# A gated product streamed through one core: the first tile in pieces, and an early copy on the scalar engine's DMA queue

## The chip, the core and the metric

The kernel runs on one core of one Trainium2 chip. The metric is the device time of one execution in microseconds (us). Before the change the median of three runs is 933.64 us (933.28 to 933.91).

The core's engines each follow their own list of instructions and meet through semaphores: ACT (the scalar engine), DVE (the vector engine), POOL, PE (no work here) and SP, which here only issues transfers. Transfers between device memory (DRAM) and on-chip memory (128 partitions) are carried by 16 DMA engines. SP and ACT each have a DMA queue of their own; both feed the same 16 engines. In the trace SP's queue is q1 and ACT's is q10.

## The reference

```python
# x: 8192 x 8192, float32
def reference(x):
    a, b = np.split(x, 2, axis=-1)
    return a * (1 / (1 + np.exp(-b)))     # 8192 x 4096, float32
```

Each row of x holds 4096 values of a and then 4096 of b; the output is a times the sigmoid of b. 268 MB are read and 134 MB written, and each value is used once.

## The kernel before

**Tiles.** A tile is 256 rows of x: two neighbouring rows in each of the 128 partitions (`R = 2`), so that a partition's part of a load is one run of 64 KB in DRAM, and its part of a store one run of 32 KB. There are 32 tiles. Inputs and outputs have two buffers each (`x_sb0`, `x_sb1`, `o_sb0`, `o_sb1`), and tile i uses buffer i mod 2.

**A tile's work.** SP issues the load (L51). ACT replaces b by its sigmoid in place (L66), DVE multiplies a by it into the output buffer (L80), and ACT issues the store (L90). Most tiles are one ACT and one DVE instruction over two rows of 4096 columns. Two tiles are cut. Tile 0 is loaded as two DMAs, one for each row of a partition, and worked as the whole first row and then three parts of the second (1024, 1024 and 2048 columns); it is stored whole. The last tile is loaded whole and worked in four parts of 2048 columns, which SP stores as four DMAs.

**Order.** The program has no scheduler; `trace` (L100 to L116) writes down the order, and the semaphores do the rest:

- `loaded0` and `loaded1` count a tile's load for each buffer, and `row` the second row of tile 0. Each DMA adds 16 when it has landed. The first sigmoid of a tile waits for `loaded`.
- `ready0` and `ready1` count, for each buffer, the first sigmoid of a tile and the landing of stores. The first multiply of tile i waits for both: its sigmoid, and the store of tile i - 2 that empties the output buffer. Later pieces of a tile wait for `sigmoid`.
- `product` counts multiplies. Load i + 2 waits until the multiplies of tile i are done, and so does the store of tile i.

A waiting instruction holds up what stands behind it on the same engine. On SP that is the order of the loads; on ACT the store of tile i stands between the sigmoids of tile i and those of tile i + 1.

**The beginning.** The program opens with a barrier between the engines (L175, L157 in the trace). `_launch_early` (L133) takes the first load, the first row of tile 0, out of the body and puts it ahead of SP's drain of that barrier, so that it is issued before the engines have met. All other DMAs are issued behind the barrier: SP goes on with the second row of tile 0 and the whole of tile 1, and ACT loads its table for the sigmoid.

**The end.** `close` (L118) drains ACT, DVE and SP; POOL waits for them and for the store of the last tile but one, and clears the semaphores. SP waits for the last four stores (L130).

Of the kernel before, what the change touches and what calls it, by code (L numbers as in the profile page):

```python
# [1 line left out]

# [4 lines left out]

P = 128
R = 2
SLOTS = 2  # L10


class _Program:

    def __init__(self, nc, x, out):
        self.nc = nc
        fp32 = mybir.dt.float32
        n_rows, n_cols = x.shape  # L30
        self.half = n_cols // 2
        self.n_tiles = n_rows // (P * R)
        self.x = x.rearrange("(n p r) m -> n p (r m)", p=P, r=R)
        self.out = out.rearrange("(n p r) m -> n p (r m)", p=P, r=R)
        self.xs = [nc.alloc_sbuf_tensor(f"x_sb{s}", [P, R * n_cols], fp32).ap() for s in range(SLOTS)]
        self.os = [nc.alloc_sbuf_tensor(f"o_sb{s}", [P, R * self.half], fp32).ap() for s in range(SLOTS)]
        self.loaded = [nc.alloc_semaphore(f"loaded{s}") for s in range(SLOTS)]
        self.ready = [nc.alloc_semaphore(f"ready{s}") for s in range(SLOTS)]
        self.product = nc.alloc_semaphore("product")
        self.sigmoid = nc.alloc_semaphore("sigmoid")  # L40
        self.row = nc.alloc_semaphore("row")
        self.arrived = nc.alloc_semaphore("arrived")
        self.last = nc.alloc_semaphore("last")
        self.to_ready, self.stored = [0] * SLOTS, [0] * SLOTS
        self.products = self.sigmoids = self.lasts = 0
        self.done = {}

    def load(self, i, rows=slice(0, R), landed=None):
        s = i % SLOTS
        part = slice(rows.start * 2 * self.half, rows.stop * 2 * self.half)  # L50
        ins = self.nc.sync.dma_start(out=self.xs[s][:, part], in_=self.x[i][:, part])  # L51
        ins.then_inc(landed or self.loaded[s], 16)
        if i >= SLOTS:
            ins._wait_ge(self.product, self.done[i - SLOTS])
        return ins

    def work(self, i, pieces):


        nc, s = self.nc, i % SLOTS  # L60
        rows = self.xs[s].rearrange("p (r h m) -> p r h m", r=R, h=2)
        packed = self.os[s].rearrange("p (r m) -> p r m", r=R)
        waits = []
        for k, (r, c) in enumerate(pieces):
            b = rows[:, r, 1, c]
            sig = nc.scalar.activation(out=b, in_=b, func=mybir.ActivationFunctionType.Sigmoid)  # L66
            if k == 0:
                sig._wait_ge(self.loaded[s], 16 * (i // SLOTS + 1))
                self.to_ready[s] += 1 + self.stored[s]
                waits.append((self.ready[s], self.to_ready[s]))  # L70
                sig.then_inc(self.ready[s], 1)
                self.stored[s] = 0
            else:
                if i == 0 and r.start == 1 and c.start == 0:
                    sig._wait_ge(self.row, 16)
                self.sigmoids += 1
                waits.append((self.sigmoid, self.sigmoids))
                sig.then_inc(self.sigmoid, 1)
        for (r, c), wait in zip(pieces, waits):
            mul = nc.vector.tensor_mul(out=packed[:, r, c], in0=rows[:, r, 0, c], in1=rows[:, r, 1, c])  # L80
            mul._wait_ge(*wait)
            mul.then_inc(self.product, 1)
            self.products += 1
        self.done[i] = self.products

    def store(self, i, lo=0, hi=None, products=None):
        s, final = i % SLOTS, i == self.n_tiles - 1
        hi = R * self.half if hi is None else hi
        queue = self.nc.sync if final else self.nc.scalar
        ins = queue.dma_start(out=self.out[i][:, lo:hi], in_=self.os[s][:, lo:hi])  # L90
        ins._wait_ge(self.product, self.done[i] if products is None else products)
        if final:
            self.lasts += 16
            ins.then_inc(self.last, 16)
        else:
            self.stored[s] += 16
            ins.then_inc(self.ready[s], 16)
        return ins

    def trace(self):  # L100

        n, half = self.n_tiles, self.half
        whole = [(slice(0, R), slice(0, half))]
        cuts = (0, half // 4, half // 2, half)
        by_row = [(slice(0, 1), slice(0, half))] + [(slice(1, 2), slice(a, b)) for a, b in zip(cuts, cuts[1:])]
        fourths = [(slice(r, r + 1), slice(h * half // 2, (h + 1) * half // 2)) for r in range(R) for h in range(2)]
        self.load(0, slice(1, 2), self.row)
        self.load(1)
        for i in range(n):
            self.work(i, fourths if i == n - 1 else whole if i else by_row)  # L110
            if i + SLOTS < n:
                self.load(i + SLOTS)
            if i < n - 1:
                self.store(i)
        for k in range(4):
            self.store(n - 1, k * half // 2, (k + 1) * half // 2, self.products - 3 + k)  # L116

    def close(self):  # L118


        nc, s = self.nc, (self.n_tiles - 2) % SLOTS
        for engine in (nc.scalar, nc.vector, nc.sync):
            engine.drain().then_inc(self.arrived, 1)  # L123
        nc.gpsimd.wait_ge(self.arrived, 3)
        nc.gpsimd.wait_ge(self.ready[s], self.to_ready[s] + self.stored[s])
        ids = sorted(h.num for h in (*self.loaded, *self.ready, self.product, self.sigmoid, self.row, self.arrived))
        assert ids == list(range(ids[0], ids[-1] + 1)) and self.last.num not in ids
        nc.gpsimd.sem_clear(range(ids[0], ids[-1] + 1))
        nc.gpsimd.drain()
        nc.sync.wait_ge(self.last, self.lasts).then_inc(self.last, -self.lasts)  # L130


def _launch_early(nc):  # L133

    SP = mybir.EngineType.SP
    entry, body = (b.instructions for b in nc.main_func.blocks[:2])
    load = next(i for i in body if i.engine == SP and i.opcode == "DMACopy")
    assert not load.sync_info.on_wait  # L140
    body.remove(load)
    where = next(k for k, i in enumerate(entry) if i.engine == SP and i.opcode == "Drain")
    entry.insert(where, load)


@with_exitstack
def kernel(
    ctx: ExitStack,
    tc: tile.TileContext,
    x: bass.AP,  # L150
    out: bass.AP,
):
    nc = tc.nc
    prog = _Program(nc, x, out)
    tc.info.no_tile_sem_insts.add(prog.load(0, slice(0, 1)).ins.name)
    tc.close()
    tc.compile()  # L157
    _launch_early(nc)
    prog.trace()
    prog.close()  # L160


# [1 line left out]
_INS = ['x']  # L164
_OUTS = [((8192, 4096), 'float32')]


# [23 lines left out]
```

## Time and profile before

The profile is of one execution. Its first instruction is SP's early load at 0.00, and its last is SP's wait for the last stores.

| what | value |
|---|---|
| median of three runs | 933.64 us |
| span of the profiled execution, first to last instruction | 932.0 us |
| moved by the DMA engines over the span | 402.67 MB, 432 GB/s |
| DVE busy, 38 instructions | 278.7 us |
| ACT busy, 39 instructions | 226.9 us |
| a sigmoid of a whole tile / of 2048 / of 1024 columns | 7.03 / 1.90 / 1.05 us |
| a multiply of a whole tile / of 2048 / of 1024 columns | 8.69 / 2.29 / 1.22 us |
| a whole load, issue to landing (median) | 42.2 us |
| a whole store, issue to landing (median) | 34.8 us |
| one of the last four stores, issue to landing (median) | 5.8 us |

How to read it: an engine's busy time says how much it works, not what the kernel waits for. DMA time from issue to landing holds the time behind other transfers on the same engines. The trace also keeps every DMA packet with its queue, start, duration and size. A packet here is one partition's run of a DMA, up to 64 KB, or one record of 4 bytes that tells a semaphore of a DMA's end; each of the 16 engines carries the packets of 8 partitions.

### The profile page before, as it was taken

To read this page: it belongs to the slowest core of one execution; us is meant where nothing else is said; L and a number is where in the kernel's file an instruction comes from. 1 tells how busy PE (TensorE), PEld (TensorE's weight loads), DVE (VectorE), ACT (ScalarE), POOL (GpSimd) and SP (SyncE) were. 2 spreads that over 40 slices of the span, in tenths; PEclk is the share of its full clock that TensorE was granted. 3 is DMA by queue.
4 is the path that set the end of the run, shared out by engine and by line. 5 is a ranking of instruction groups with operands and counts; after the bars stand their busy time and mean duration, and the time that the engine had idled before them with its cause. 6 is when DMAs were issued, how large, how long until landed. Compare 5 with 4: busy or idle time off the path is not lost.

```text
span 932.0 us, 191 instructions
## 1 busy us (share of the span) xinstructions
DVE 278.7 (30%) x38; ACT 226.9 (24%) x39; POOL 0.2 (0%) x4
## 2 busy tenths in 40 slices
DVE  2133213332133331233312333123331233312333
ACT  2133330233311333113331133311333113332033
POOL 0000000000000000000000000000000000000000
DMA  9999999999999999999999999999999999999999
GB/s 405 418 460 428 408 461 413 450 428 428 450 405 450 428 428 450 428 428 428 461 416 428 436 464 428 405 458 419 450 428 425 453 405 450 428 428 450 423 432 405
DMA packets 9793, 402.67 MB, mean 432 GB/s; under 512 B 1088, under 2 KB 1088, under 8 KB 1088
## 3 DMA queue, kind: packets, MB, share of 16 engines
q1 hardware_dynamic: 5328, 272.63, 67.7%
q10 hardware_dynamic: 4464, 130.03, 32.3%
q14 instruction: 1, 0.01, 0.0%
HBM read 268.44 MB, written 134.22 MB: 432 GB/s over the span
## 4 chain that ended last, share of the span: by engine, by line
DMA 73%; DVE 15%; ACT 12%; DVEq 0%; issue 0%; SPq 0%
DMA x_sb<-in_x_dram 73%; DVE o_sb L80 15%; ACT x_sb L66 12%; DVEq L123 0%; SPq L51 0%
## 5 line engine op out<-in xcount | busy, mean ns | idle before, releaser
L80 DVE TENSOR_TENSOR o_sb<-x_sb 128x8192 f32<-128x8192 f32 (+3 forms) x38 | 278.7, 7344 | 647.1 <-ACT x_sb L66 647.1
L66 ACT ACTIVATE x_sb<-x_sb 128x8192 f32<-128x8192 f32 (+3 forms) x38 | 225.6, 5949 | 693.9 <-DMA x_sb<-in_x_dram 693.9
L66 ACT ACT_TABLE_LOAD x1 | 1.3, 1283 | 1.4 <-PEq L157 1.4
L175 POOL MEMSET const-bfloat16-1.0<- 128x1 bf16 x1 | 0.1, 101 | 0.0
L175 POOL MEMSET const-uint8-127<- 128x1 uint8 x1 | 0.1, 101 | 0.0
L175 POOL MEMSET const-float32-0.0<- 128x1 f32 x1 | 0.1, 98 | 0.2 <-issue 0.2
L175 POOL MEMSET const-float32-1.0<- 128x1 f32 x1 | 0.1, 98 | 0.0
## 6 DMA issues: line engine op xcount, KB each, us to landing
out_dram<-o_sb ACTq DMA_DIRECT2D x31, 4096.0 KB, 34.8
x_sb<-in_x_dram SPq DMA_DIRECT2D x2, 4096.0 KB, 16.2
out_dram<-o_sb SPq DMA_DIRECT2D x4, 1024.0 KB, 5.8
x_sb<-in_x_dram SPq DMA_DIRECT2D x31, 42.2
```

Of the source, the lines that this page charges most:

```text
L66: sig = nc.scalar.activation(out=b, in_=b, func=mybir.ActivationFunctionType.Sigmoid)
L80: mul = nc.vector.tensor_mul(out=packed[:, r, c], in0=rows[:, r, 0, c], in1=rows[:, r, 1, c])
L175: nc = _bacc.Bacc("TRN2", target_bir_lowering=False, num_devices=1)
```

## The change

The first tile is loaded as four DMAs, worked in five pieces and stored as four DMAs. A piece of columns takes the same columns of both halves, a and b. The first of these loads is the one that stands ahead of the barrier. The first three pieces are 1024, 1024 and 2048 columns of a partition's first row; the fourth load is the whole second row, which is worked in two pieces of 2048 columns and stored at once.

ACT gets a DMA of its own ahead of the barrier, in front of its drain: 16 rows of 512 bytes are copied from x in DRAM to the output in DRAM, in rows that belong to tile 1. They hold no result; the store of tile 1 overwrites them later, and ACT waits for the copy's end (`opened`) ahead of that store.

ACT issues each of the first tile's stores right behind the sigmoid of that piece, so that it waits there for the piece's multiply. In the other tiles nothing changes. The semaphore `row` gives way to three for the parts of tile 0 and one for the copy.

```diff
+FIRST = [(ROW0, slice(0, 1024)), (ROW0, slice(1024, 2048)), (ROW0, slice(2048, 4096)), (ROW1, slice(0, 4096))]
+FIRST_WORK = FIRST[:3] + [(ROW1, slice(0, 2048)), (ROW1, slice(2048, 4096))]
+FIRST_STORES = [(0, 1024, 0), (1024, 2048, 1), (2048, 4096, 2), (4096, 8192, 4)]
+
+def FIRST_LANDINGS(part):
+    return (*part, None)
...
+    def load_part(self, k):
+        r, c = FIRST[k]
+        both = lambda ap: ap.rearrange("p (r h m) -> p r h m", r=R, h=2)[:, r, :, c]
+        ins = self.nc.sync.dma_start(out=both(self.xs[0]), in_=both(self.x[0]))
+        return ins.then_inc(self.part[k - 1] if k else self.loaded[0], 16)
+
+    def opening(self):
+        rows = slice(P * R, P * R + 16)
+        ins = self.nc.scalar.dma_start(out=self.flat_out[rows, 0:128], in_=self.flat_x[rows, 0:128])
+        return ins.then_inc(self.opened, 16)
...
-                if i == 0 and r.start == 1 and c.start == 0:
-                    sig._wait_ge(self.row, 16)
+                if k <= len(landings) and landings[k - 1] is not None:
+                    sig._wait_ge(landings[k - 1], 16)
...
+            for lo, hi, upto in stores or ():
+                if upto == k:
+                    self.store(i, lo, hi, first + k + 1)
...
-        self.load(0, slice(1, 2), self.row)
+        for k in range(1, len(FIRST)):
+            self.load_part(k)
         self.load(1)
         for i in range(n):
-            self.work(i, fourths if i == n - 1 else whole if i else by_row)
+            if i == 0:
+                self.work(0, FIRST_WORK, FIRST_LANDINGS(self.part), FIRST_STORES)
+            else:
+                self.work(i, fourths if i == n - 1 else whole)
             if i + SLOTS < n:
                 self.load(i + SLOTS)
-            if i < n - 1:
+            if i == 1:
+                self.nc.scalar.wait_ge(self.opened, 16)
+            if 0 < i < n - 1:
                 self.store(i)
...
 def _launch_early(nc):
     entry, body = (b.instructions for b in nc.main_func.blocks[:2])
-    load = next(i for i in body if i.engine == SP and i.opcode == "DMACopy")
...
+    for engine in (mybir.EngineType.SP, mybir.EngineType.Activation):
+        first = next(i for i in body if i.engine == engine and i.opcode == "DMACopy")
+        assert not first.sync_info.on_wait
+        body.remove(first)
+        where = next(k for k, i in enumerate(entry) if i.engine == engine and i.opcode == "Drain")
+        entry.insert(where, first)
```

## The prediction

> **What bounds the kernel now.** I read the page's slices first, then the windows, the waits, the timeline at both ends, and last the single DMA packets that the trace keeps. The page:
>
> ```profile
> span 932.0 us, 191 instructions
> ## 1 busy us (share of the span) xinstructions
> DVE 278.7 (30%) x38; ACT 226.9 (24%) x39; POOL 0.2 (0%) x4
> ...
> DMA  9999999999999999999999999999999999999999
> ...
> q1 hardware_dynamic: 5328, 272.63, 67.7%
> q10 hardware_dynamic: 4464, 130.03, 32.3%
> ```
>
> No compute engine is busy a third of the time, and the 16 DMA engines are busy in every slice; the two queues' shares add to 100%. q1 is SP's queue (loads, and the last tile's stores), q10 is ACT's (all other stores). Windows (columns: length, busy time of DVE, ACT and POOL, clock, DMA share, GB/s) show whether an end is different:
>
> ```profile
> 0.00:30.00 30.00, 9.08 (x4) 8.70 (x5) 0.20 (x4) 1.00 0.99 419
> 30.00:60.00 30.00, 5.54 (x1) 7.03 (x1) 0.00 (x0) 1.00 1.01 419
> ...
> 119.00:177.00 58.00, 17.38 (x2) 14.06 (x2) 0.00 (x0) 1.00 1.00 434
> ...
> 920.00:925.00 5.00, 5.00 (x3) 2.26 (x2) 0.00 (x0) 1.00 0.99 421
> ```
>
> The first 30 us, with loads alone in flight, have the same DMA share as the middle, with loads and stores: the engines don't care which they carry. ACT waits for loads and DVE for ACT:
>
> ```profile
> ACT x_sb L66 <- DMA x_sb<-in_x_dram: 693.9, 33, 22.2
> DVE o_sb L80 <- ACT x_sb L66: 647.1, 34, 26.5
> ```
>
> So earlier arithmetic is worth nothing by itself; only DMA time counts: bytes, packets, and moments when an engine moves nothing. The bytes stay the same (but for 8 KB). The packets, followed engine by engine: the first start at 1.00 to 1.84 us, the last end at 931.1 to 931.6, and between them an engine's gaps come to less than 0.02 us in any 5 us. A 64 KB packet takes 2.418 us (median), a 32 KB one 1.213, an 8 KB one 0.309. Only two groups took longer: the first 16 on q1, one per engine (+0.62 us on the mean), and 16 on q1 that start at 30.66 to 31.10, again one per engine: 3.55 to 3.75 us in place of 2.42, **a stall of 1.23 us on every engine**. Right behind each of these comes q10's very first packet (34.31 to 34.76). The store that opens q10 was issued at 28.00:
>
> ```profile
> 0.00 28.33 SPq L51 DMA_DIRECT2D x_sb<-in_x_dram  x4
> ...
> 1.44 1.28 ACT L66 ACT_TABLE_LOAD   x1 [1.44 <-PEq L157]
> 12.12 3.62 ACT L66 ACTIVATE x_sb<-x_sb 128x4096 f32<-128x4096 f32 x1 [9.41 <-DMA x_sb<-in_x_dram]
> ...
> 28.00 0.38 ACTq L90 DMA_DIRECT2D out_dram<-o_sb  x1
> ```
>
> SP issues its four loads of that first row at 0.00, 1.43, 1.81 and 28.00.
>
> **The change part by part.**
>
> *More, smaller packets: +0.45 us.* One DMA engine serves 8 of 128 partitions. Tile 0 costs it now 16 load packets of 32 KB and 8 store packets of 32 KB, 24 in all. After: a piece of 1024 columns is two runs of 4 KB in each partition (the a half and the b half), so 16 + 16 packets of 4 KB and 16 of 8 KB for the first row; the second row is one run of 32 KB, 8 packets; the stores are 8 each of 4, 4, 8 and 16 KB: 88 in all, 64 more. Neighbouring starts within a queue are 2.413 us apart at 64 KB and 0.3064 at 8 KB, which makes 27.2 GB/s and a constant of 0.0055 us a packet. 64 x 0.0055 = 0.35. Six more DMAs (9 in place of 3 for tile 0 and the copy) write a completion record each, 9 ns by the rows of 4 bytes: 0.05. The 512-byte packet of the copy is taken at 0.05. No 4 KB packet is in this trace; the nearest row, 8 KB, lies on the line through the others to 1%, so I keep 0.3 to 0.6.
>
> *The scalar engine's copy: between -1.23 and 0, taken as -0.65.* If the 1.23 us are the price of q10's first use, the copy pays it near 1 us instead of 31. There it is free as far as the engines have nothing to do yet (before 1.00 to 1.84) or are in the 0.62 us that q1's first packets lose anyway. Whether two first uses run side by side, no row shows. Side by side they cost nothing more (-1.23); one behind the other everything (0); the middle is -0.6, and I lean a little to the gain since q10's request leaves ACT at about the moment that SP's leaves SP. On ACT the issue stands ahead of the barrier: ACT's drain is at 0.13 now, SP's ends at 0.55 and POOL gathers them at 0.58. An issue of 0.38 (the store at 28.00) ends within that; the longest issue in the trace, 0.81, would move the barrier, and SP's next load with it, by some 0.4. The table load behind it has until the first piece lands.
>
> *The first tile's loads: 0, if the supply holds.* Piece 0 keeps an engine for 16 x 0.156 = 2.5 us: from 1.13 (mean first start) + 0.62 to 4.25. Piece 1 is issued at 1.43, behind the barrier; from issue to first packet the first load took 1.00 to 1.84, so it is there by 3.3, or 3.7 with the late barrier. Pieces 2 and 3 and tile 1 follow some 0.4 us apart, and from 4.25 each holds far more than that. The cover now is 4 MB deep (9.7 us); after, it is 1 MB with 0.6 us to spare.
>
> *Earlier stores: 0.* Piece 0 lands near 5, ACT takes 1.05 and DVE 1.22, so the first store is issued near 7.3 instead of 28. It moves no byte more: each store packet only pushes load packets back. On ACT's queue each store now waits for its product ahead of the next sigmoid (1.2 to 2.3 us each); pieces land 2.5, 6 and 10 us apart, so that hides. The trace shows the two queues taking turns packet by packet (64 KB of q1, 32 KB of q10, and so on), so tile 0's 32 small store packets now need 32 turns in place of 8. Counting the turns: the store of tile 0 has landed at about 73 (now 61.4), load 1 at 46 (now 47.4), load 2 at 70 (now 73.9). The multiply of tile 2, which needs tile 0's output buffer, starts not before 70 + 7.03 = 77, so it isn't held. From there the stores trail further: load 30 to landing of store 29 some 30 us instead of 21.6.
>
> *The tail: 0.* When load 31 lands at 914.93 its engines still hold seven 32 KB packets of store 30, up to 921.8, and the first store of the last tile, issued at 919.21, starts at 921.3 to 921.9:
>
> ```profile
> 914.95 7.31 ACT L66 ACTIVATE x_sb<-x_sb 128x2048 f32<-128x2048 f32 x4 [21.88 <-DMA x_sb<-in_x_dram]
> 916.89 8.90 DVE L80 TENSOR_TENSOR o_sb<-x_sb 128x2048 f32<-128x2048 f32 x4 [15.10 <-ACT x_sb L66]
> 919.21 6.94 SPq L90 DMA_DIRECT2D out_dram<-o_sb  x4
> ```
>
> This cover is used up to the last packet today. Stores that trail further make it thicker; there is no gap to win back. If the cover were thinner, every us would be lost.
>
> Sum: 0.45 - 0.65 = -0.2. The span of 932.0 becomes 931.8; the median of the runs shown is 933.64, 1.64 above that span, so **933.4 us**, with 932.8 to 934.2 as this case's own range: no change. A measurement of this kernel can tell some 0.2%, 1.87 us, from nothing.
>
> [...]
>
> **The rivals.**
>
> *The supply breaks (slower).* At one place, piece 0 to piece 1, engines stand still if piece 1's first packet comes more than 4.25 - 1.43 = 2.8 us behind its issue. For: store 1, issued at 63.18, had its first packet at 68.14, 4.96 later, and piece 1 has twice the descriptors. Against: that was a busy engine with two packets of 2.41 us picked ahead, and the same queue's first load needed 1.0 to 1.84. With 4.96, piece 1 starts at 6.39: 2.1 us lost, the copy hidden as before: 2.1 + 0.45 - 0.65 = +1.9, 935.5. Chance 0.13.
>
> *The copy opens nothing.* The 1.23 us may belong to the first store out of SBUF, not to the queue; then it comes again near 9 us. 933.64 + 0.45 = 934.1; within no change. Chance 0.2.
>
> *The copy is hidden whole.* 0.45 - 1.23 = -0.8: 932.85; within no change. Chance 0.25. To come below 931.77 the change would need 1.87 us, and the trace has 1.23 + 0.62 of stalls in all, less 0.45 of packets; for something that it doesn't show I leave 0.07.
>
> *Each DMA pays its latency.* If the engines drained between DMAs, each of six would cost 5.8 - 2.45 = 3.3 us (landing less packets of a 1 MB store): +20, 953. [...] The gapless tail speaks against it: 0.02.
>
> **How the numbers follow.** Forecast (part of the stall saved) 0.33, hidden whole 0.25, opens nothing 0.2: together no change, 0.78. Slower 0.13 + 0.02 = 0.15, faster 0.07. The range takes 932.3 to 935.0: the three same cases with 0.3 us of spread between runs on either side, and the smaller breaks of supply.
>
> **What would show it.** Right: no packet near 31 us of over 2.45 us; the first packets on both queues by 3 us; starts of piece 1 right behind piece 0; four-KB packets of 0.155 to 0.165 us; a first store issued near 7; store 29 landing about 30 us behind load 30; the end as gapless as now. Wrong: a gap on all engines near 4 us (supply), a stall of 1.2 us behind the first real store (nothing opened), first load packets 1.2 us later than now (one behind the other), or a gap near 920 us.

## The result, and the profile after

The changed kernel takes 941.35 us (median of 4 runs, 940.46 to 944.13), the kernel before 933.77 in the same comparison: a ratio of 1.0089 (95% interval 1.0076 to 1.0102). It is slower by 7.6 us where no change was forecast, and outside the range. The profiled execution has a span of 939.1 us, 7.1 more than before. Its page:

```profile
span 939.1 us, 200 instructions
...
DVE 278.9 (30%) x39; ACT 227.2 (24%) x40; POOL 0.2 (0%) x4
...
DMA  9999999999999999999999999999999999999997
...
q1 hardware_dynamic: 6000, 272.63, 67.3%
q10 hardware_dynamic: 4928, 130.03, 32.1%
```

The work is the same, and the DMA engines are as busy as before, but for the last slice. Windows of the changed kernel (length, DVE, ACT, POOL, clock, DMA share, GB/s):

```profile
0.00:30.00 30.00, 6.04 (x4) 8.55 (x6) 0.20 (x4) 1.00 1.00 402
30.00:60.00 30.00, 7.62 (x3) 7.50 (x2) 0.00 (x0) 1.00 1.00 430
119.00:177.00 58.00, 17.39 (x2) 14.06 (x2) 0.00 (x0) 1.00 1.00 434
915.00:923.00 8.00, 2.62 (x2) 4.56 (x3) 0.00 (x0) 1.00 0.82 352
923.00:926.00 3.00, 3.00 (x2) 2.75 (x2) 0.00 (x0) 1.00 0.84 350
...
934.00:939.00 5.00, 0.00 (x0) 0.00 (x0) 0.00 (x0) 1.00 0.09 36
```

The middle runs at 434 GB/s, as before. The end doesn't: in the last 5 us a share of 0.09 is little more than one engine of 16. The waits and the two ends of the timeline:

```profile
DVE o_sb L91 <- DMA out_dram<-o_sb: 18.7, 1, 18.7
```

```profile
0.00 3.55 SPq L59 DMA_DIRECT2D x_sb<-in_x_dram  x4
0.12 0.63 ACTq L65 DMA_DIRECT2D out_dram<-in_x_dram  x1
...
5.66 1.06 ACT L78 ACTIVATE x_sb<-x_sb 128x1024 f32<-128x1024 f32 x1 [2.32 <-DMA x_sb<-in_x_dram]
...
8.01 0.36 ACTq L103 DMA_DIRECT2D out_dram<-o_sb  x1
...
72.66 7.03 ACT L78 ACTIVATE x_sb<-x_sb 128x8192 f32<-128x8192 f32 x1 [17.12 <-DMA x_sb<-in_x_dram]
82.97 8.69 DVE L91 TENSOR_TENSOR o_sb<-x_sb 128x8192 f32<-128x8192 f32 x1 [18.71 <-DMA out_dram<-o_sb]
```

```profile
918.44 7.31 ACT L78 ACTIVATE x_sb<-x_sb 128x2048 f32<-128x2048 f32 x4 [22.17 <-DMA x_sb<-in_x_dram]
920.38 8.90 DVE L91 TENSOR_TENSOR o_sb<-x_sb 128x2048 f32<-128x2048 f32 x4 [15.39 <-ACT x_sb L78]
922.70 6.94 SPq L103 DMA_DIRECT2D out_dram<-o_sb  x4
```

The beginning is as forecast to within a microsecond: first store at 8.01 instead of 28.00. But the last load lands at 918.4 instead of 914.9, and tile 2's multiply had to wait for tile 0's store.

The page averages over the 16 engines, so it can't show what happened; the packets can. Each engine ends its share of a DMA with a record of 4 bytes (some 9 ns; 16 of them to a DMA). The times of the first and the last of the 16 records of a load (tile 0's are called piece or row, load 1 is that of tile 1, and so on):

```
                before            after
first load      11.2 to 11.8      4.5 to 5.2     (before: row 0; after: piece 0)
next            21.0 to 21.4      7.3 to 9.3     (before: row 1; after: piece 1)
load 1          46.4 to 46.8      44.8 to 48.1
load 3          102.0 to 102.4    93.5 to 101.3
load 31         914.0 to 914.5    906.8 to 918.1
```

**The engines have fallen out of step.** Before, all 16 do the same thing within half a us (0.45 to 0.54), all through the run. After, they are 7.8 us apart at load 3 and 11.3 at load 31, and a load has landed only when its slowest engine is done: the sigmoid behind load 31 starts at 918.44, after the last record. At the end most engines ran dry: they stood still for 1.7 us on the mean (0.5 to 2.3) until the last tile's first store came (near 923.6), and 14 ended near 933.6, 2.3 us later than before (931.3). The other two ended at 936.36 and 938.78. On two engines the 64 KB packets had also become slower, by some 4 and 6 us in sum after 40 us; before, no engine lost over 0.3.

### The profile page after: what moved, and what is told of

It reads as the page before. It is cut to its first block, busy times and chain, and to the rows that moved or that the text cites. A ratio compares the mean times of both kernels' runs of the same rounds, so it can differ in the third digit from the quotient of the medians.

```text
span 939.1 us, 200 instructions
## 1 busy us (share of the span) xinstructions
DVE 278.9 (30%) x39; ACT 227.2 (24%) x40; POOL 0.2 (0%) x4
## 4 chain that ended last, share of the span: by engine, by line
DMA 71%; DVE 15%; ACT 12%; DVEq 0%; SPq 0%; issue 0%
DMA x_sb<-in_x_dram 71%; DVE o_sb L91 15%; ACT x_sb L78 12%; DVEq L139 0%; SPq L59 0%
## 5 line engine op out<-in xcount | busy, mean ns | idle before, releaser
L91 DVE TENSOR_TENSOR o_sb<-x_sb 128x8192 f32<-128x8192 f32 (+2 forms) x39 | 278.9, 7160 | 650.4 <-ACT x_sb L78 631.7
L78 ACT ACTIVATE x_sb<-x_sb 128x8192 f32<-128x8192 f32 (+2 forms) x39 | 225.9, 5802 | 696.5 <-DMA x_sb<-in_x_dram 696.5
```

## The experiments

Theory A: an offset between engines is kept in turns (a turn is one packet of q1 and one of q10). While a turn is 4 and 8 KB, two turns are less than 1 us; when it is 64 and 32 KB, 3.62 us by the packets' durations, two turns are 7.2. So a small unevenness, caught by small early stores, would grow. The rivals, B to D, stand in the expectations of the runs. Each run's ratio is to the kernel before in the same comparison.

**The copy alone.** Tile 0 as before, with the copy:

```diff
-FIRST = [(ROW0, slice(0, 1024)), (ROW0, slice(1024, 2048)), (ROW0, slice(2048, 4096)), (ROW1, slice(0, 4096))]
+FIRST = [(ROW0, slice(0, 4096)), (ROW1, slice(0, 4096))]
-FIRST_STORES = [(0, 1024, 0), (1024, 2048, 1), (2048, 4096, 2), (4096, 8192, 4)]
+FIRST_STORES = [(0, 8192, 3)]
```

> Tile 0 as in the kernel before; only the 512-byte copy ahead of the barrier is added. In the changed kernel the 16 DMA engines end a load up to 11 us apart (0.5 us before), and most of the loss is taken to be that. Theory A (the engines fall out of step because small packets of loads and stores meet at unequal turns): no pieces, so the engines stay within 0.5 us, the stall of 1.23 us near 31 us is gone, and the time is 0.3 to 1.2 us below the kernel before (932.5 to 933.5). Theory B (the copy is to blame: its issue of 0.63 us holds up the barrier, and it opens q10 at an unlucky moment): the engines fall out of step here too and the time is 937 or more.

933.32 us against 933.17, ratio 1.0001 (0.9992 to 1.001): no change. The engines stay within 0.7 us. The stall near 31 us is still there: 1.03 us on each engine, 1.23 before. The copy opens next to nothing, and it does no harm (B falls). A had expected the stall to be gone, and it is not.

**The pieces alone.** The changed kernel without `opening()`.

> The changed kernel without the copy: loads, work and stores of tile 0 in pieces. Theory A: the engines still fall out of step (load 30 lands over 6 us or more from first to last engine) and the time is 938 to 944. Theory B: without the copy SP's second load is issued at 1.43 again rather than 2.06, piece 1 arrives in time, the engines stay within 1 us of each other, and the time is 933.5 to 935.

946.25 us (940.65 to 951.87), ratio 1.0139 (1.0095 to 1.0184). The four executions lie apart, two near 941.6 and two near 951; the trace is of one at 950.02. There load 30 lands 9.7 us apart from first engine to last, and the 64 KB packets are slow on all engines, by 9.3 us in sum on the mean engine. The pieces (loads and stores) are the cause, and piece 1's landing is 1.4 us apart even with SP's second load on time, so the late barrier is at most a part of the uneven start.

**Tile 0 stored whole; loads in pieces.**

```diff
-FIRST_STORES = [(0, 1024, 0), (1024, 2048, 1), (2048, 4096, 2), (4096, 8192, 4)]
+FIRST_STORES = [(0, 8192, 4)]
```

> The changed kernel, but tile 0 is stored as one DMA of 32 KB packets behind its last piece; loads in pieces and the copy stay. Theory A in its full form (an offset between engines that is counted in turns is kept while a turn grows from 4 + 8 KB to 64 + 32 KB, so it is the small early stores that blow up 2 us of unequal start to 7 to 11 us): the spread of the landings stays at about 2.5 us, at most one turn (3.6 us), and the time is 934.5 to 937. Theory C (the unequal start of the small loads is the loss, whatever the stores): the spread is 6 us or more and the time 938 or more.

934.3 us, ratio 1.0012 (1.0003 to 1.0021). Loads land 1.6 us apart, from piece 1 to the end, and don't grow beyond 2.8. The same uneven start, without the small stores, costs 1.1 us: it is the small stores that make the offset large, as A has it (the time came out just below its range), and C falls.

**Tile 0 stored in pieces; loads as before.** Two loads of 32 KB packets, no copy, the changed kernel's work and stores.

> Loads as in the kernel before (two rows of 32 KB packets, no copy), but tile 0 is worked and stored in the changed kernel's pieces, so that the stores of 4, 4, 8 and 16 KB packets meet loads of 32 and 64 KB. Theory A: the engines are in step when the stores join, so all keep the same turns; spread below 1 us, time within 0.5 us of the kernel before (933.3 to 934.3). Theory D (small store packets pull the engines apart by themselves): spread of 5 us or more, time 938 or more.

935.89 us, ratio 1.003 (1.0018 to 1.0042): between the two ranges. The engines keep within 0.4 us until load 4 is issued, so D falls; but another wait appears, here in the waits of this run:

```profile
DVE o_sb L91 <- DMA out_dram<-o_sb: 31.4, 1, 31.4
```

Tile 0's 32 small store packets need 32 turns against packets of 64 KB. The store lands at 89.9, and tile 2's multiply, which needs its output buffer, starts at 90.26. Load 4 and store 2 are issued behind it at 98.98; by then load 3 (86.8) and store 1 (99.5) are at their ends, and the engines stand still for about 1 us. The expectation had not reckoned with this wait. One engine then comes out some 3 us late.

**Two engines made late.** The kernel before, with a copy of 128 KB that only two engines carry:

```diff
+        some = lambda t: t[P * R:P * R + 128, :].rearrange("(a b) m -> a b m", a=2)[:, 0:4, 0:self.half]
+        ins = self.nc.scalar.dma_start(out=some(self.flat_out), in_=some(self.flat_x))
```

> The kernel before, with one DMA ahead of the barrier that gives two of the 16 engines, and only these, 64 KB more to copy from DRAM to DRAM (4 packets of 16 KB each, about 2.4 us of one engine by the rows of 16 KB packets, 0.611 us each). The copied rows are overwritten by tile 1's store. Theory A1 (an engine that falls behind stays behind and sets each landing and the end, nothing more): these two engines land every load some 2.4 us later than the others, or 3.6 if they lose one turn, and the end comes 2.4 us later: 935.2 to 936.5. Theory A2 (an engine out of step is also slowed further at each tile, as the two latest of the changed kernel seem to be, 0.2 us a tile): the gap grows along the run and the time is 937 or more. If lateness were made up by the waits of other engines: no change, 933.2.

935.98 us, ratio 1.003 (1.0019 to 1.0041): A1. The two engines land 2.9 us behind the first one at load 0, 4.0 at load 1, and still 4.7 at load 31. Lateness is kept to the end, and no other engine takes over work of the late two; but being out of step does not by itself make packets slow (0.2% of the load packets).

**Two early stores.** Loads as before; tile 0's rows stored one by one.

```diff
+FIRST_WORK = [(ROW0, slice(0, 4096)), (ROW1, slice(0, 2048)), (ROW1, slice(2048, 4096))]
+FIRST_STORES = [(0, 4096, 0), (4096, 8192, 2)]
```

> Loads as in the kernel before, no copy; tile 0's first row stored by itself as soon as it is worked, the second row behind it: two stores of 16 KB packets. In the run with early stores of 4 to 16 KB, tile 0's store landed so late (89 us) that tile 2's multiply waited for the output buffer and both DMA queues ran dry near 100 us; here 16 turns in place of 32 let it land by about 65. Theory (engines in step, no dry queue): spread of landings below 1 us and 932.5 to 934. Rival (any early store costs, by its turns): 935 or more, like the four small stores.

963.18 us, ratio 1.0314 (1.0287 to 1.0341): far above what the theory gave, and far more than the four small stores cost. No multiply waits for its buffer and the engines start in step. What is slow is the load packets: a quarter of them take longer, by 0.41 us on the mean, some 24 us for each engine.

**Brought together again.** The changed kernel; load 2 waits until tile 0's stores have landed.

```diff
+            if i == 0:
+                self.nc.sync.wait_ge(self.ready[0], 1 + self.stored[0])
             if i + SLOTS < n:
                 self.load(i + SLOTS)
```

> The changed kernel, pieces and copy and all, with one wait more: SP issues load 2 only when all of tile 0's stores have landed. Both queues run out once, so that all 16 engines start load 2 at the same moment. This costs some 2 to 4 us of idle engines near 57 us. Theory A (the loss is that the engines go out of step in the first 30 us and stay so): from load 2 on the landings lie within 1 us again, no packet is slow, and the time is 934.5 to 938 in spite of the idle time, below the changed kernel's 941.35. Rival (the loss lies in the small packets and the late start themselves): the idle time comes on top, 943 or more.

939.05 us, ratio 1.0061 (1.0047 to 1.0074): 1 us above A's range, and lower than the changed kernel although all engines stand still near 52 us. The spread is 1.9 us (1 was expected). The engines stand still for 2.6 us on the mean, the first packets behind that lose 1.6 us an engine, and later no load packet is slow. With the 1.1 us of the loads in pieces this makes 5.3 of the 5.9 us. So the large offset and the slow packets of the changed kernel are gone, and most of what is left is the price of the wait: this speaks for A.

**Loads in pieces, two stores.** The changed kernel with `FIRST_STORES = [(0, 4096, 2), (4096, 8192, 4)]`.

> The changed kernel with its copy and its loads in pieces, but tile 0 stored as two DMAs of 16 KB packets (the first row behind its third piece, the second behind its last). With one whole store the time was 934.3 and the engines 1.6 us apart; with four small ones 941.35 and up to 11 us. Theory A in its form of turns: the first store joins at about 20 us, when the loads of the second row (32 KB packets) are under way and the engines are 2.6 us, about two turns of 32 KB, apart; the offset of one to two turns becomes 3.6 to 7 us: 936 to 939. Rival (only packets of 4 and 8 KB do harm): 934 to 935.

934.35 us, ratio 1.0011 (1.0002 to 1.0021): below the 936 to 939 that A gave, and within the range of its rival. The spread is 2.6 us and no packet is slow. But that only packets of 4 and 8 KB do harm doesn't hold either: the same two stores cost 30 us behind whole loads and 1.1 here. So neither size nor number of the stores decides by itself.

**What these runs have in common.** Following each engine's packets through the runs so far, I counted where its stores stand against its loads: by how many turns the store of tile k ends behind the load of tile k + 2. (The queues take turns, and a completion record takes a turn of its own: in the kernel before one engine carries a store packet at 245.76, a load's record at 246.97, the next store packet at 246.98. So two loads in a row mark the end of a store and two stores in a row the end of a load. Engines that coincide can be taken for each other.)

```
position             run: load packets slowed by over 15 ns
2 turns ahead        kernel before: 0%; tile 0 stored whole: 0%; together again: 0%
1 turn ahead         pieces with two stores: 0%; two engines late: 0%
level                stores in pieces, whole loads: 1%; changed kernel: 0%
                     pieces alone: 36%; two early stores: 30%
1 turn behind        changed kernel: 18%; pieces alone: 21%; two early stores: 22%
2, 3, 4 behind       changed kernel: 0% each; pieces alone: 0%, 0%, 3%
```

In the changed kernel the engines are spread from level to four turns behind, and the delayed packets are those of the engines at one turn. Theory P: the position of the store stream makes the packets slow. The row "level" shows that this can't be the whole rule. With stores in pieces all 16 engines stand level from load 4 to the end, and next to nothing is slow; with two early stores they come to level late in the run (all 16 by load 29), and over 40% of the packets of loads 29 and 30 are slow.

**A late store.** The kernel before, with nothing but a wait that holds tile 0's store back:

```diff
+            if i == 0:
+                self.nc.scalar.wait_ge(self.loaded[1], 16)
             if i < n - 1:
                 self.store(i)
```

> The kernel before, with one wait more: ACT issues the store of tile 0 only when load 1 has landed (near 41 us in place of 28). No piece, no small packet, no copy; the stores only trail the loads by some turns more. In the kernel before store k lands 7.3 us ahead of load k + 2 and no packet is slow; in the run with two early stores it landed 3.3 us behind load k + 2, and a quarter of all 64 KB load packets took 0.43 us longer on the mean, 25 us for each engine. Theory P (what makes packets slow is by how many turns the stores trail the loads, however that came about): with 3 or 4 turns more than before the load packets are slow here too, and the time is 940 to 965. Rival (small packets, or stores that begin early, are needed): no slow packets, 933 to 934.5.

952.64 us, ratio 1.021 (1.0192 to 1.0228). The store leaves at 41.19, all engines come to stand one turn behind, and 22% of the load packets are slow:

```profile
41.19 0.38 ACTq L90 DMA_DIRECT2D out_dram<-o_sb  x1
```

The window from 600 to 900 us of this run (the last column is GB/s) beside that of the kernel before:

```profile
600.00:900.00 300.00, 86.93 (x10) 70.29 (x10) 0.00 (x0) 1.00 1.01 427
```

```profile
600.00:900.00 300.00, 93.82 (x11) 73.16 (x11) 0.00 (x0) 1.00 1.00 433
```

A busy share of 1.0 in both, and 6 GB/s less: the busy share counts a slow packet like a quick one, so it can't show the loss. The rival that small packets are needed falls. One engine's packets around the end of a tile, with start, L for load or s for store, KB, and the ns over the median (records left out):

```
late store:  240.1 s32  241.3 L64  243.7 s32  244.9 s32  246.1 L64  248.6 L64  251.0 s32  252.2 L64 +308  254.9 s32  256.1 L64 +164
before:      240.0 L64  242.4 s32  243.7 L64  246.1 s32  247.3 s32  248.5 L64  250.9 s32  252.1 L64  254.5 s32  255.7 L64
```

Delayed are nearly only the second and the third packet of a load (58% and 86% of these; of the others 25% at most, 0 to 6% for most), those right behind the place where the ends of a load and of a store follow each other.

**Later in ACT's order, without a wait.** The store of tile 0 behind tile 1's sigmoid on ACT:

```diff
+            if i == 1:
+                self.store(0)
-            if i < n - 1:
+            if 0 < i < n - 1:
                 self.store(i)
```

> The kernel before, but the store of tile 0 is issued behind the sigmoid of tile 1 (near 48 us in place of 28), so that the stores trail by some 6 to 7 turns more than before. In the changed kernel the two engines whose stores landed together with load k + 2 had slow packets, and those whose stores trailed furthest (16 us behind load k + 2) had nearly none. Theory P in its narrow form (only some positions of the store stream against the load stream are slow): less slow than with a store at 41 us, 933.5 to 940, with a wait of a multiply for its output buffer in the first tiles. Theory P in its wide form (any trailing past load k + 2 is slow): 945 or more.

952.89 us, ratio 1.0211 (1.0195 to 1.0228), the same as the late store, since it was the same: the sigmoid started at 41.19 and ACT issued the store at 41.20, beside it. So it tells nothing of later positions.

```profile
41.19 7.03 ACT L66 ACTIVATE x_sb<-x_sb 128x8192 f32<-128x8192 f32 x1 [15.55 <-DMA x_sb<-in_x_dram]
41.20 16.14 ACTq L90 DMA_DIRECT2D out_dram<-o_sb  x2
```

**Still later, with a wait for the sigmoid's end.**

```diff
+            if i == 1:
+                self.nc.scalar.wait_ge(self.ready[1], 1)
+                self.store(0)
-            if i < n - 1:
+            if 0 < i < n - 1:
                 self.store(i)
```

> As the run with the late store of tile 0 (issued at 41 us: 952.6 us, stores one turn behind, 22% of the load packets slow), but ACT also waits for the end of tile 1's sigmoid, so that this store is issued near 48.3 us. The attempt to do this without that wait issued it at 41.2 and only repeated the late store. Counted engine by engine over the runs so far, load packets are slow where the store of a tile ends one turn behind the load two tiles on (13 to 24% of the packets), and not where it ends two turns ahead, one ahead, level, or two to four behind (0 to 3%). Theory N (only the position one turn behind is slow): three turns more, no slow packets, 933.5 to 937 although the store is later still. Theory W (any trailing is slow): 948 or more.

**933.42 us**, ratio 1.0 (0.999 to 1.001). The store leaves at 48.18, all engines stand three to four turns behind, and no more than 1% of the load packets are slow. Seven microseconds later than the late store, and 19 us quicker: of the two theories, N. So being late is not what costs, and the position alone, with nothing else changed, can cost 19 us. N's further claim, that only this one position is slow, does not hold for the level engines above. The store's issue (the first of two in the row) and the waits of this run:

```profile
48.18 9.03 ACTq L90 DMA_DIRECT2D out_dram<-o_sb  x2
```

```profile
DVE o_sb L80 <- DMA out_dram<-o_sb: 603.5, 30, 26.7
```

Thirty multiplies wait for their output buffers, 603 us in all, and it costs nothing, since the DMA engines do not run dry: busy in every slice of this run's page, 432 GB/s over the span.

**On-chip and device addresses.** The run with two early stores, first with the output buffers exchanged (`self.os[1 - s]`), then with loads 1 to 30 taken 10 rows further on in x (so that it computes from other rows):

> The run with two early stores (963 us), with the two output buffers exchanged: even tiles use the second one, odd tiles the first; order and waits are the same. If the slow packets come from on-chip addresses (a load that writes one buffer while the store reads its partner), the slow packets change: the time moves by over 10 us. If they come from device memory or from the order alone, nothing changes: 958 to 968.

> The run with two early stores (963 us), with all loads but those of the first and the last tile taken from 10 rows (320 KB) further on in x; order, sizes and waits are the same, and the output is not the reference's. If the slow packets come from the places in device memory that loads and stores use at the same moment, the share of slow packets changes: the time moves by over 10 us, most likely down. If they come from the order alone, 958 to 968.

960.77 us (ratio 1.0293, 1.0269 to 1.0317) and 960.98 (1.0278, 1.0226 to 1.033): as slow as without, with mostly the second and third packets of a load slow again at one turn behind, and 18 and 20% of the packets at level. These two changes of address do not matter; others were not tried.

**The same partition in neighbouring turns.** The late store with loads and stores cut into partitions 0 to 63 and 64 to 127:

```diff
-        ins = self.nc.sync.dma_start(out=self.xs[s][:, part], in_=self.x[i][:, part])
+        for half in (slice(0, P),) if i == 0 else (slice(0, P // 2), slice(P // 2, P)):
+            ins = self.nc.sync.dma_start(out=self.xs[s][half, part], in_=self.x[i][half, part])
```

> The late store run (952.6 us) with each load and store but those of tile 0's load and the last tile's store cut into two DMAs by partitions, 0 to 63 and then 64 to 127, loads and stores in the same order. Each engine still carries 8 packets of each tile. It is the reference for the run with crossed halves: if nothing but the cut is changed, the stores trail by about one turn as before and packets stay slow: 942 to 956.

> As the run with halves in the same order, but each store takes partitions 64 to 127 first and 0 to 63 second, so that at one turn behind an engine never loads and stores the same partition within neighbouring turns. Theory S (a load packet is slow when the engine stores that same on-chip partition in a neighbouring turn): few slow packets, 933.5 to 938, well below the run with halves in the same order. Theory T (it is the order of turns alone, whatever the partition): as slow as that run, within 4 us.

1520.39 us (1421.21 to 1534.12) and 1551.17 us (1536.27 to 1554.42): the cut itself makes both another kernel, and the question stays unanswered. A 64 KB load packet takes 4.53 us here (median, loads and stores in the same order) instead of 2.42, and a 32 KB store packet 1.42 instead of 1.21: factors of 1.87 and 1.17. Why the cut slows the packets, and the loads more than the stores, is not shown.

What makes the packets slow stays open. That the ends of a load and of a store follow each other closely is not enough: with the stores in pieces all engines stand level, both ends in the same turn by the count, and 1% of the packets is slow. No run here isolates the cause.

## Why the prediction was wrong, step by step

- **More, smaller packets, +0.45 us: right in kind.** 4 KB store packets take 0.159 us, inside the expected 0.155 to 0.165. The first 4 KB load packets take 0.206 on the mean: 1.5 us over the median in sum for each engine, where the first packets before lost 0.62. The copy's 512-byte packets took 0.027 us each, one to an engine, where the sum had put 0.05. With tile 0 stored whole or in two, the loads in pieces cost 1.1 us in all.
- **The copy, -0.65: wrong, nothing.** The rival that it opens nothing was right: with the copy alone 1.03 of the 1.23 us stay. In the run with the store at 48 us the stall comes to 1.2 us again, at that store. In the changed kernel it is absent, but so it is with the pieces alone (0.01 us ahead of the first store), so the copy is not what removed it; with two early stores the load packets ahead of the first store lose 0.3. Why is open.
- **The first loads' supply, 0: half wrong.** ACT's issue took 0.63 us and SP's second load left at 2.06, 0.63 later than before. It broke on some engines (some 0.3 us between 2 and 7 us on the mean, about 1 on the worst), not on all. I had looked for a loss shared by all; what came was an unevenness of 2 us.
- **Earlier stores, 0: the step that failed.** Its argument was that each store packet only pushes load packets back. It treated 16 engines as one, and packet durations as given. What the runs showed in its place: the same loads and copy with tile 0 stored whole cost 1.1 us, and with the four early stores 7.6, with the engines 7.8 us apart at load 3 and 11.3 at load 31 in place of 1.6. That the engines keep their distance in turns fits this (two turns of 3.6 us are 7.2), but it is argued, and with two stores it gave too much. And how far the stores trail can make load packets slow, as the late store shows (22% of them, 952.64 us). The counted landings show the first miss: load 1 48.1 for 46, load 2 72.3 for 70, tile 0's store 82.6 for 73, so that tile 2's multiply, said not to be held, started at 82.97, 3.3 us behind its sigmoid's end.
- **The tail, 0: wrong.** Before, the last four stores lie on each engine within 921.3 to 931.6 us with gaps under 0.01 us, though each takes 5.4 to 6.1 us from issue to landing, so DMAs that queue behind each other did not pay for it one by one. After, the stores trail as counted: store 29 has landed 30.4 us behind load 30. But that makes a cover only on an engine that trails. The last load lands with the slowest engine, and the engines that are ahead run dry by then.

The sum as measured, from the profiled execution: +2.3 us until most engines end (933.6 against 931.3), in which lie the rough start and the dry time at the end, and 5.2 more until the last one does (938.8; before, the last one ended at 931.6). That is about what the slowest engine lost to slow packets (some 6). That a shift of the stores alone can make packets slow is shown by the late store and the still later one; that it is this engine's position is counted from its packets, not separately tried, and what slows a packet at that position stays open.

None of the runs beats the kernel before by what can be measured.

## What to carry to other kernels

Each of the 16 DMA engines carried the same share here (248 load packets of 64 KB in the kernel before), and none took over from the two made late. So look at the engines one by one before you cost a change of packets or order at its bytes: an offset that small early packets left behind grew here from 2 us to 11, and the slowest engine set each landing (load 31: 906.8 us on the first, 918.1 on the last). This kernel's steady, DMA-bound loop ran at a rate that depended on where the store stream stood against the load stream; shifting one early store from 41.19 to 48.18 us, and nothing else, moved the time from 952.64 to 933.42 us, by 2%. Try two or three such positions before you judge a change that moves the start.

## What the runs showed of the hardware

- With all engines' stores one turn behind the load two tiles on, 22% of the 64 KB load packets were slow, by 0.32 us on the mean (the run with the late store). In the other runs counted, with the stores one or two turns ahead, or two to four behind, 0 to 3% were. Level was quick in two runs (0 and 1%) and slow in four (18 to 36%), so the position is not the whole rule.
- An engine's lateness was neither made up nor spread: two engines with an estimated 2.4 us more to carry near the start (4 packets of 0.611 us) were 4.7 us late at the last load (the run with two engines made late).
- In DMAs over 64 of the partitions a 64 KB load packet took 4.53 us, against 2.42 over all 128 (the run with halves in the same order, and the kernel before).
- ACT issued a DMA that stands behind a sigmoid as soon as that sigmoid had begun (41.20 behind 41.19); with a wait for its end it left at 48.18 (the runs with the later and the still later store).
